# Opening of the stick-breaking stage reordered in a fused transformer layer

## The chip, the cores and the metric

The kernel runs on one core of a Trainium2 chip. Its time is the device time of one execution in microseconds (us), smaller is better. TensorE (PE) multiplies, VectorE (DVE), ScalarE (ACT) and GpSimd (POOL) work on tiles, and SyncE (SP) issues nearly all transfers, which run on 16 DMA engines. Each engine takes its instructions strictly in the order in which they were put down; engines wait for each other by semaphores.

## The reference, cut to what matters

One decoder layer on 1024 tokens of width 1024. The mixer has two attention families; the second, stick-breaking attention, is the place of the change, and the modulation vector `mod` is what the small weight tiles in it are for:

```python
mod = jax.nn.silu(c) @ ada_w[layer] + ada_b[layer]
shift1, scale1, gate1, shift2, scale2, gate2 = ...split(mod, 6)
...
# stick-breaking, 8 heads, blocks of 128 queries
z = einsum('bqhd,bshd->bhqs', qb, k) * scale
log_keep = where(mask, log_sigmoid(-z), 0.0)
suffix = cumsum(log_keep, reverse=True) - log_keep
a = where(mask, exp(log_sigmoid(z) + suffix), 0.0)
y_b = einsum('bhqs,bshd->bqhd', a, v)
...
h = h + gate1 * ((sigmoid(m_a) * y_a + sigmoid(m_b) * y_b) @ w_out)
h = h + gate2 * (square(relu(u2 @ mlp_w1)) @ mlp_w2)
```

All products are made from float32 values split into a high and a low part, so one product is three matmuls.

## The kernel before, in words

The program is one long stream: normalisation and input projection, sparse attention (`nsa_all`), stick-breaking attention (`sb_gens`), up-projection, output projection, MLP. A part of the input projection, 28 units of 48 matmuls of 128x512 (line L748, called filling products below, written to the banks `pd`), is kept back and laid between the matmuls of both attention stages, so that PE has work while their other engines are busy. `drive` draws filling products in proportion to the estimated cost of each attention step, `pump` draws a stretch of them at once. Finished units are copied out (`zo`, L1023) and stored to `z_d` in memory, from which the stick-breaking stage and the up-projection load them again.

The stick-breaking stage works head by head. For head h, `prep` loads its query and key rows (`zr`), casts the query tile `Q` on ACT (L1080), makes its low part and the key tiles `Kh`, `Kl` on POOL. `prep_v` takes the value rows of two heads (`vr`), transposes them on PE (L1098), casts them to `V` on ACT (L1102) and makes the low part on DVE (L1104). Then come twelve score chunks per head, in three groups of four (`sb_a`): two or three matmuls into a score bank `psx` (L1128 to L1131), a sigmoid into `sig` and a sigmoid in place on ACT (L1133, L1134), a running product from right to left on DVE into `Pt` (L1143), a multiplication on POOL (L1145). There are three banks `psx`, so the matmuls of chunk n+3 wait for the running product of chunk n. One group later the results are transposed on PE (`turn`, L1160), split on ACT and DVE (L1168, L1169) and multiplied with `V` (L1180).

`ada_rest(sp, (3,), ...)` makes one row of `mod` on the side: 32 steps, each loading a 128x256 tile `adraw` of `ada_w` on SP (L423), scaling it on ACT (L443) and adding it on POOL (L447). A buffer of `adraw` is free again after the addition. `side(1)` asks for one step; the first call only issues as many loads as there are buffers.

The order within each engine is not the order of the code alone: when the program is built, a scheduler plays it through on estimated times and lets any instruction that it thinks ready go ahead on its engine. The manual dependence in `behind` holds filling products behind the attention matmuls, and is off while `pump` runs.

Of the kernel before, what the change touches and what calls it, by code (L numbers as in the profile page):

```python
# [6 lines left out]
F32 = mybir.dt.float32  # L7
F32R = mybir.dt.float32r
BF16 = mybir.dt.bfloat16
AF = mybir.ActivationFunctionType  # L10
# [25 lines left out]
def build(tc, I, out):  # L36
    nc = tc.nc
# [65 lines left out]
    def po(name="po"):  # L103
# [7 lines left out]
                            fill=0.0, base=0, channel_multiplier=1)  # L111
    ones = const.tile([128, 128], F32, name="ones")
# [301 lines left out]
    def ada_rest(pool_, rows, ahead, engines, W=512):  # L414
        groups = [(r, h) for r in rows for h in range(D // W)]
        total = len(groups) * NK
        nxt = []

        def load(n):
            r, h = groups[n // NK]  # L420
            raw = pool_.tile([128, W], F32, name="adraw", bufs=ahead)
            c0 = (2 + r) * D + h * W
            nc.sync.dma_start(raw, ada_k[:, n % NK, c0:c0 + W])  # L423
            nxt.append(raw)

        for n in range(min(ahead, total)):
            load(n)
        yield
        for n in range(total):
            raw = nxt.pop(0)  # L430
            k = n % NK
            (r, h), w, e = groups[n // NK], cs[:, k:k + 1], engines[n // NK % len(engines)]
            if k == 0:
                acc = pool_.tile([128, W], F32, name="adacc", bufs=1)
            if e == "v":
                if k == 0:
                    nc.vector.tensor_scalar(acc, raw, w, None, op0=OP.mult)
                else:
                    nc.vector.scalar_tensor_tensor(acc, raw, w, acc, op0=OP.mult, op1=OP.add)
            else:  # L440
                d = acc if k == 0 else raw
                if e == "s":
                    nc.scalar.mul(d, raw, w)  # L443
                else:
                    nc.gpsimd.tensor_scalar(d, raw, w, 0.0, op0=OP.mult, op1=OP.add)
                if k:
                    nc.gpsimd.tensor_tensor(acc, acc, raw, op=OP.add)  # L447
            if n + ahead < total:
                load(n + ahead)
            if k == NK - 1:  # L450
                nc.sync.dma_start(acc_d[r][:, h * W:(h + 1) * W], acc)
            yield

    adp = pool("adp", "left")
    ada_steps = ada_rest(adp, (1, 2), 2, "v")

    def side(n):
        for _ in range(n):
            next(ada_steps, None)
# [269 lines left out]
    def track(ins):  # L729

        last[:] = [ins.ins]
# [7 lines left out]
    def unit_mm(w, sink):  # L739
        wh, wl = w  # L740
        pend = None
        for h in range(2):
# [3 lines left out]
            for k in range(NK):  # L746
                for n, (a, b) in enumerate(((wh[:, k], uH(k, sl)), (wh[:, k], ul[:, k, sl]), (wl[:, k], uH(k, sl)))):
# [4 lines left out]
                    if m == 3 and pend:  # L752
# [13 lines left out]
                            fill=NEG, base=0, channel_multiplier=-1)  # L766
# [6 lines left out]
                            fill=NEG, base=0, channel_multiplier=1)  # L773
# [240 lines left out]
    TAIL = 96  # L1014
# [24 lines left out]
    def drive(main, fill, ratio, extra=0.0, keep=0):  # L1039

        debt = 0.0
        for c in main:
            debt += c * ratio + extra
            while debt > 0 and left[0] > keep:
                m = next(fill, None)
                if m is None:
                    break
                debt -= m

    def pump(fill, us):  # L1050

        free[0] = 1
        while us > 0:
            m = next(fill, None)
            if m is None:
                break
            us -= m
        free[0] = 0


    def sb_gens(sp):
        zero = sp.tile([128, 128], F32, name="zero")[:, 0:1]
        nc.vector.memset(zero, 0.0)

        def load(u, h):
            zr = sp.tile([128, S], F32, name="zr", bufs=2)
            for r in range(2):
                nc.sync.dma_start(zr[r * HD:(r + 1) * HD], z_d[u][(h % 2) * HD:(h % 2 + 1) * HD, :])
            return zr

        def load_v(p):
            vr = sp.tile([128, S], F32, name="vr", bufs=1)
            nc.sync.dma_start(vr, z_d[8 + p])
            return vr
# [16 lines left out]

        def prep_v(vr, V):
            tv = [sp.tile([128, NT, 2, HD], F32R, name="V", bufs=3) for _ in range(2)]
            for q in range(2):
# [11 lines left out]
                yield 0.0  # L1106
            V.extend(tv)

# [62 lines left out]

        def times_v(V):
            h, g, kt, c0, th, tl = split_.pop(0)
# [5 lines left out]
            for q, t_ in enumerate((th, tl)):  # L1179
                track(nc.tensor.matmul(p[:, c0:], V[h][:, kt].rearrange("p s d -> p (s d)"), t_[:, c0:],  # L1180
                                       start=kt == top and q == 0, stop=kt == 0 and q == 1, skip_group_check=True))
# [8 lines left out]
        def sb_all():  # L1190
            lds = {0: (load(0, 0), load(4, 0))}
            vr = load_v(0)
            ops = {}
            for r in prep(0, lds[0]):
                ops[0] = r
            V = []
            for c in prep_v(vr, V):
                yield c
            groups = [(h, kind) for h in range(8) for kind in range(3)]
            A, edges, late = {}, {}, []  # L1200
            extra = []
            for k in range(len(groups) + 1):
                if k < len(groups):
                    h, kind = groups[k]
                    if kind == 0:
                        A[h, 0] = {}
                        if h + 1 < 8:
                            lds[h + 1] = (load((h + 1) // 2, h + 1), load(4 + (h + 1) // 2, h + 1))
                            if h % 2 == 1:
                                vr = load_v((h + 1) // 2)  # L1210
                    if kind == 1:
                        A[h, 1] = {}
                        if h + 1 < 8:
                            extra.append(prep(h + 1, lds[h + 1]))
                            if h % 2 == 1:
                                extra.append(prep_v(vr, V))
                    chunks = chunks_of(kind)
                for c in range(4):
                    cost = 0.0
                    if k < len(groups):  # L1220
                        fin, cost = sb_a(kind, chunks[c], ops[h], A[h, min(kind, 1)], edges)
                        late.append(fin)
                        yield cost
                    if len(late) > 1 or k == len(groups):
                        if late:
                            late.pop(0)()
                    cost = 0.0
                    if k > 0:
                        hb, kb = groups[k - 1]
                        g = min(kb, 1)  # L1230
                        cost += turn(hb, g, (3, 7, 3)[kb] - c, A[hb, g])

                        if split_ and (wait[0] or split_[0][2] != 4 * split_[0][1] + 3):
                            while len(split_) > 0:
                                cost += times_v(V)
                            wait[0] = 0
                        elif split_:
                            wait[0] = 1
                        if len(turned) > 1:
                            halves()  # L1240
                    yield cost
                    if c % 2:
                        side(1)
                    for e in list(extra):
                        r = next(e, "end")
                        if r == "end":
                            extra.remove(e)
                        elif isinstance(r, tuple):
                            ops[h + 1] = r
                        elif r:  # L1250
                            yield r
                if k < len(groups) and kind == 2:
                    for e in extra:
                        for r in e:
                            if isinstance(r, tuple):
                                ops[h + 1] = r
                            elif r:
                                yield r
                    extra = []
            while turned or split_:  # L1260
                cost = 0.0
                while split_:
                    cost += times_v(V)
                if turned:
                    halves()
                yield cost
# [78 lines left out]
    fill = fill_all()  # L1345
    pump(fill, 25.0)
    drive(nsa_all(), fill, 0.4, 0.05)
    pump(fill, 20.0)
    close(at)
    close(bnp)  # L1350
    close(kvp)
    sp = pool("sb", "right")
    ada_steps = ada_rest(sp, (3,), 2, "s", 256)
    drive(sb_gens(sp), fill, 0.55, 0.08, TAIL)
    for _ in ada_steps:
        pass
    close(sp)
# [39 lines left out]
    ada_steps = ada_rest(yb, (0,), 2, "s")  # L1397
# [367 lines left out]
```

## Time and profile before

| | us |
|---|---|
| median of three runs (lowest 1712.92, highest 5434.21) | 1713.28 |
| the profiled execution | 1711.0 |
| its span, first to last instruction | 1709.3 |
| PE busy in it | 1646.8 |
| DVE, POOL, ACT busy | 1276.9, 948.8, 875.7 |

The profiled execution is 1.7 us longer than its span; the median is 2.3 us above the profiled execution. The profile's times count from the start of the span. A PE busy for 96% of the span can gain from a change off PE only where it stands still or where its granted clock is down.

### The profile page before, as it was taken

What the parts mean: (1) busy time and instruction counts of PE and PEld (TensorE: products, weight loads), DVE (VectorE), ACT (ScalarE), POOL (GpSimd) and SP (SyncE); (2) the same over time, 40 slices, a digit from 0 to 9 for tenths busy, and PEclk for the clock granted to TensorE, in tenths of its full rate; (3) what the DMA queues carried; (4) which work ended last, traced back from release to release, by engine and by line L of the source; (5) the groups of instructions that cost most, each with busy time, mean ns of one, the idle gap of its engine ahead of it and who ended that gap; (6) DMA issues with size and microseconds to landing.
All of it is one profiled execution on the core that took longest, in us unless ns stands there. A gap on an engine that the chain in (4) does not pass through costs nothing.

```text
span 1709.3 us, 25308 instructions
## 1 busy us (share of the span) xinstructions
PE 1646.8 (96%) x8484; PEld 1384.8 (81%) x8484; DVE 1276.9 (75%) x2614; ACT 875.7 (51%) x1898; POOL 948.8 (56%) x837
## 2 busy tenths in 40 slices
PE   5999999999999989999999999899999999999998
PEld 4879888888888877878778888778788888888886
DVE  7598477778877648778745546679888888979887
ACT  6434376666666547776554435543444443453442
POOL 0021134343434368775316302399889897989897
PEclk9999999999999999999999999999999999999999
DMA  9366311111211164451187443865373654636232
GB/s 306 106 177 177 97 56 55 57 55 50 61 45 50 38 180 126 114 139 51 38 287 235 155 176 116 279 232 211 119 273 104 243 200 157 243 116 269 99 148 99
DMA packets 159386, 245.22 MB, mean 143 GB/s; under 512 B 15432, under 2 KB 109336, under 8 KB 150296
## 3 DMA queue, kind: packets, MB, share of 16 engines
q1 hardware_dynamic: 155032, 241.51, 42.6%
q10 hardware_dynamic: 4224, 2.10, 0.4%
q8 instruction: 67, 1.10, 0.3%
q14 instruction: 63, 0.52, 0.1%
HBM read 203.71 MB, written 39.86 MB: 142 GB/s over the span
## 4 chain that ended last, share of the span: by engine, by line
PE 75%; POOL 7%; DVE 6%; DMA 5%; ACT 3%; issue 3%; SPq 0%; POOLq 0%; DVEq 0%; ACTq 0%
PE pd L748 16%; PE psx L1705 10%; PE pd L1639 7%; PE pt L1639 5%; PE px L1329 5%; PE po L913 5%; PE px L1441 4%; PE pt L947 4%; PE po L1705 3%; POOL raw L1679 3%; DMA adraw<-in_ada_w_dram 2%; PE psx L829 2%; PE psx L830 2%; PE po L1180 1%; POOL wbl L1681 1%
## 5 line engine op out<-in xcount | busy, mean ns | idle before, releaser
L1708 DVE TENSOR_TENSOR acc<-acc,psx 128x512 f32<-128x512 f32 x288 | 178.8, 675 | 8.0 <-PE psx L1705 7.9
L748 PE MATMUL pd<-uh,uwh 128*128 128x512 f32 x448 | 181.4, 405 | 0.7 <-ACT zo L1023 0.7
L748 PE MATMUL pd<-ul,uwh 128*128 128x512 f32 x448 | 178.0, 397 | 0.0
L748 PE MATMUL pd<-uh,uwl 128*128 128x512 f32 x448 | 177.0, 395 | 0.0
L66 DVE TENSOR_TENSOR wl<-aw,wh 128x1024 fp32r<-128x1024 f32 x49 | 115.1, 2349 | 65.8 <-ACT wh L61 65.8
L1679 POOL TENSOR_TENSOR raw<-r 128x512 f32<-128x512 f32 x80 | 131.3, 1659 | 32.1 <-ACT r L1614 32.0
L1705 PE MATMUL psx<-wbl,rah 128*128 128x512 f32 x336 | 131.3, 391 | 4.2 <-POOL wbl L1681 3.0
L1705 PE MATMUL psx<-wbh,rah 128*128 128x512 f32 x336 | 130.8, 391 | 1.9 <-ACT wbh L1680 1.5
L1705 PE MATMUL psx<-wbh,ral 128*128 128x512 f32 x336 | 131.0, 390 | 0.1
L905 DVE TENSOR_TENSOR tl<-pt,th 128x512 fp32r<-128x512 f32 (+8 forms) x168 | 103.6, 619 | 34.5 <-ACT th L904 33.4
L1681 POOL TENSOR_TENSOR wbl<-raw,wbh 128x1024 fp32r<-128x1024 f32 x40 | 109.1, 2728 | 19.5 <-ACT wbh L1680 19.5
L904 ACT CAST th<-pt 128x512 fp32r<-128x512 f32 (+8 forms) x168 | 88.7, 530 | 61.0 <-PE pt L947 59.0
L886 POOL TENSOR_TENSOR pcx<-pcx,tot 128x64 f32<-128x64 f32 (+7 forms) x32 | 10.5, 329 | 172.2 <-DVE tot L884 95.3
L63 POOL TENSOR_SCALAR uwh<-uwr 128x512 fp32r<-128x512 f32 x54 | 33.5, 628 | 123.2 <-PE pd L748 96.7
L1667 POOL TENSOR_TENSOR w<-w,grow 128x1024 f32<-128x1024 f32 x32 | 95.0, 2991 | 11.8 <-DVE aw L1595 11.8
L748 PEld LDWEIGHTS pd<-uh,uwl 128*128 128x128 f32 x448 | 85.0, 190 | 17.8
L1680 ACT CAST rah<-raw 128x1024 fp32r<-128x1024 f32 x40 | 41.4, 1050 | 111.7 <-PE po L1705 58.8
L748 PEld LDWEIGHTS pd<-uh,uwh 128*128 128x128 f32 x448 | 85.3, 190 | 14.9 <-ACT zo L1023 1.1
L748 PEld LDWEIGHTS pd<-ul,uwh 128*128 128x128 f32 x448 | 85.3, 190 | 13.2
L1639 PE MATMUL pd<-mth,wl 128*128 128x512 f32 x224 | 87.6, 392 | 0.8 <-DVE wl L66 0.8
L1639 PE MATMUL pd<-mth,wh 128*128 128x512 f32 x224 | 87.8, 392 | 0.6 <-ACT wh L61 0.6
L1639 PE MATMUL pd<-mtl,wh 128*128 128x512 f32 x224 | 87.8, 392 | 0.0
(361 smaller groups left out, 5352.5 us busy)
## 6 DMA issues: line engine op xcount, KB each, us to landing
mtl<-t_d SPq DMA_DIRECT2D x35, 1024.0 KB, 5.8
mth<-t_d SPq DMA_DIRECT2D x35, 1024.0 KB, 8.2
w<-in_mlp_w_dram SPq DMA_DIRECT2D x32, 512.0 KB, 6.1
z_d<-zo SPq DMA_DIRECT2D x56, 256.0 KB, 2.0
aw<-in_mlp_w_dram SPq DMA_DIRECT2D x28, 512.0 KB, 4.2
uwr<-in_w_in_dram SPq DMA_DIRECT2D x54, 256.0 KB, 3.0
adraw<-in_ada_w_dram SPq DMA_DIRECT2D x48, 256.0 KB, 3.0
xa<-in_ada_w_dram SPq DMA_DIRECT2D x32, 256.0 KB, 5.7
```

What stands on the lines that cost most here:

```text
L66: (nc.vector if e == "v" else nc.gpsimd).tensor_tensor(dst, src, f(h), op=OP.subtract)
L748: r = nc.tensor.matmul(p, a, b, start=(k == 0 and n == 0), stop=(k == NK - 1 and n == 2))
L904: nc.scalar.copy(th[:rows, :w], p[:rows, :w])
L905: nc.vector.tensor_tensor(tl[:rows, :w], p[:rows, :w], f(th)[:rows, :w], op=OP.subtract)
L913: track(nc.tensor.matmul(po_[:, :256], w, tt[q][:rows, m * 256:(m + 1) * 256], start=(n == 0 and m == 0 and q == 0), stop=(n == last and m ...
L1329: nc.tensor.matmul(p, a, b, start=(k == 0 and n == 0), stop=(k == 3 and n == 2))
L1639: nc.tensor.matmul(bank[ft], a[:, k, fs], b[k], start=(k == 0 and m == 0 and not on), stop=(k == 3 and m == 2), skip_group_check=on)
L1667: nc.gpsimd.tensor_tensor(W2[c][j], W2[c][j], grow2, op=OP.mult)
L1679: nc.gpsimd.tensor_tensor(d, block(i0, j0, s), block(i1, j1, s), op=OP.add if sg > 0 else OP.subtract)
L1681: (nc.vector if e == "v" else nc.gpsimd).tensor_tensor(l.rearrange("p s n -> p (s n)"), src, f(h).rearrange("p s n -> p (s n)"), op=OP.sub ...
L1705: nc.tensor.matmul(p, a[:, s, qs], b[:, s], start=(s == 0 and n == 0), stop=(s == 1 and n == 2))
L1708: nc.vector.tensor_tensor(acc[:, t, ds_], acc[:, t, ds_], p, op=OP.add if sg > 0 else OP.subtract)
```

## The change

The stage is opened in steps. The filling products that were drawn in one stretch of 20 us ahead of the stage are drawn as 4 us ahead of it, 8 us after the first head's query and key preparation, and 8 us after the value preparation, which is now written in one piece. Right after the first loads are issued, a sigmoid of one column (`warm`) is written, so that the table of sigmoid is loaded there. The modulation row has eight buffers `adraw` where it had two; its first loads are issued with the value preparation, and the group of the first head's first four chunks asks for no steps.

```diff
-        zero = sp.tile([128, 128], F32, name="zero")[:, 0:1]
+        zero = sp.tile([128, 128], F32, name="zero")
+        warm, zero = zero[:, 1:2], zero[:, 0:1]
         nc.vector.memset(zero, 0.0)
...
             vr = load_v(0)
+
+            nc.scalar.activation(warm, ones[:, 0:1], AF.Sigmoid)
             ops = {}
             for r in prep(0, lds[0]):
                 ops[0] = r
+            yield 0.0
             V = []
             for c in prep_v(vr, V):
-                yield c
+                pass
+            side(1)
+            yield 0.0
...
-                    if c % 2:
+                    if k > 0 and c % 2:
                         side(1)
...
-    pump(fill, 20.0)
+    pump(fill, 4.0)
...
-    ada_steps = ada_rest(sp, (3,), 2, "s", 256)
-    drive(sb_gens(sp), fill, 0.55, 0.08, TAIL)
+    ada_steps = ada_rest(sp, (3,), 8, "s", 256)
+    sb = sb_gens(sp)
+    for us in (8.0, 8.0):
+        next(sb)
+        pump(fill, us)
+    drive(sb, fill, 0.55, 0.08, TAIL)
```

On ACT, from the last step of sparse attention to the second score chunk, the order before is this (`sig_...` with its number is one tile of `sig`):

```order
L960 COPY otmp<-po 64x256
L1023 COPY zo<-pd 128x512
L1080 CAST Q<-zr 128x1024
L1023 COPY zo<-pd 128x512
L443 ACTIVATE adacc<-adraw,cs 128x256
L443 ACTIVATE adraw<-adraw,cs 128x256
L1080 CAST Q<-zr 128x1024
L443 ACTIVATE adraw<-adraw,cs 128x256
L1102 CAST V<-pt 128x4x64 x2
L443 ACTIVATE adraw<-adraw,cs 128x256
L1102 CAST V<-pt 128x4x64 x2
L1133 ACT_TABLE_LOAD
```

After the change the same stretch of ACT reads:

```order
L1195 ACT_TABLE_LOAD
L1195 ACTIVATE zero<-ones 128x1
L1023 COPY zo<-pd 128x512
L1081 CAST Q<-zr 128x1024
L443 ACTIVATE adacc<-adraw,cs 128x256
L1023 COPY zo<-pd 128x512
L443 ACTIVATE adraw<-adraw,cs 128x256 x7
L1103 CAST V<-pt 128x4x64 x4
L1081 CAST Q<-zr 128x1024
L1134 ACTIVATE sig_8461<-psx 128x512
L1135 ACTIVATE psx<-psx 128x512
L443 ACTIVATE adraw<-adraw,cs 128x256 x2
```

The table load moved ahead of the copy `zo`; eight scalings of `adraw` in place of four stand ahead of the first sigmoid, and two more between the first chunk's sigmoids and the second's.

On SP, from the first loads of the stage on, the order before is:

```order
L1068 DMA zr<-z_d 64x1024 x4
L1024 DMA z_d<-zo 128x512 x2
L1073 DMA vr<-z_d 128x1024
L710 DMA uwr<-in_w_in_dram 128x4x128 x2
L423 DMA adraw<-in_ada_w_dram 128x256 x2
L1068 DMA zr<-z_d 64x1024 x2
L1024 DMA z_d<-zo 128x512
L710 DMA uwr<-in_w_in_dram 128x4x128
L423 DMA adraw<-in_ada_w_dram 128x256
L1068 DMA zr<-z_d 64x1024 x2
```

And after (`uwr` is the raw weight of a filling unit, whose buffer is free after the DVE instruction on `uwl`, L66):

```order
L1069 DMA zr<-z_d 64x1024 x4
L1024 DMA z_d<-zo 128x512
L1074 DMA vr<-z_d 128x1024
L1024 DMA z_d<-zo 128x512
L423 DMA adraw<-in_ada_w_dram 128x256 x8
L1069 DMA zr<-z_d 64x1024 x2
L1024 DMA z_d<-zo 128x512
L710 DMA uwr<-in_w_in_dram 128x4x128 x2
L1069 DMA zr<-z_d 64x1024 x2
L423 DMA adraw<-in_ada_w_dram 128x256 x4
```

Eight loads of `adraw` now go out in one row ahead of the second head's first `zr`, and the next four stand behind two `uwr` and two `zr`.

On PE, at the first score chunks, four transposes of `vr` stood three filling products ahead of the first score matmul before; now all eight stand 16 filling products ahead of it, and the rows between the chunks read, in the changed kernel:

```order
L1132 MATMUL psx<-diagr,identr 128x128
L748 MATMUL pd<-ul,uwh 128x512
L748 MATMUL pd<-uh,uwl 128x512
L1129 MATMUL psx<-Kh,Q 128x128
L1130 MATMUL psx<-Kl,Q 128x128
L1132 MATMUL psx<-diagr,identr 128x128
L1129 MATMUL psx<-Kh,Q 128x512
L1130 MATMUL psx<-Kl,Q 128x512
L1132 MATMUL psx<-diagr,identr 128x128
L748 MATMUL pd<-uh,uwh 128x512
```

The fourth chunk (128x128) and the fifth still follow each other with no filling product between them.

## Rows read from the trace of the kernel before

**Rows 1.** The page's busy times, share of the span and instructions of each engine.

```profile
PE 1646.8 (96%) x8484; PEld 1384.8 (81%) x8484; DVE 1276.9 (75%) x2614; ACT 875.7 (51%) x1898; POOL 948.8 (56%) x837
```

**Rows 2.** Stretches: length, busy PE, PEld, DVE, ACT, POOL, granted clock, DMA, GB/s.

```profile
625.70:630.94 5.24, 0.00 (x0) 0.00 (x1) 2.03 (x4) 4.72 (x10) 4.33 (x4) 0.82 0.98 301
630.94:635.68 4.74, 4.74 (x14) 3.94 (x15) 3.22 (x7) 3.92 (x10) 4.36 (x7) 0.50 0.58 151
...
642.70:645.20 2.50, 0.81 (x6) 0.40 (x4) 2.50 (x5) 1.27 (x6) 0.90 (x1) 1.00 0.80 192
645.20:650.00 4.80, 4.80 (x18) 4.02 (x19) 4.80 (x12) 3.89 (x9) 4.72 (x6) 0.64 0.10 35
650.00:856.00 206.00, 196.59 (x1071) 163.04 (x1070) 156.89 (x304) 137.38 (x318) 131.84 (x139) 0.98 0.34 94
...
892.00:895.30 3.30, 3.30 (x9) 2.61 (x8) 1.11 (x2) 0.72 (x1) 3.30 (x3) 0.50 0.84 254
```

**Rows 3.** PE in order of time: start, length, instruction, idle time before and releaser.

```profile
622.28 0.39 PE L1128 MATMUL psx<-Kh,Q 128*128 128x512 f32 x1
...
625.30 0.39 PE L748 MATMUL pd<-uh,uwl 128*128 128x512 f32 x1
630.94 0.47 PE L1128 MATMUL psx<-Kh,Q 128*128 128x128 f32 x1 [5.25 <-DVE Pt L1143]
...
644.28 0.33 PE L1128 MATMUL psx<-Kh,Q 128*128 128x128 f32 x1 [1.23 <-DVE Pt L1143]
...
645.18 0.50 PE L1128 MATMUL psx<-Kh,Q 128*128 128x512 f32 x1 [0.47 <-DVE Pt L1142]
...
891.18 0.50 PE L1329 MATMUL px<-oh,wh 128*128 128x512 f32 x1 [2.62 <-ACT wh L61]
```

**Rows 4.** ACT in order of time, at the opening of the stage.

```profile
607.46 0.58 ACT L1023 COPY zo<-pd 128x512 f32<-128x512 f32 x1 [3.74 <-PE pd L748]
...
619.71 0.51 ACT L443 ACTIVATE adacc<-adraw,cs 128x256 f32<-128x256 f32 x1 [5.20 <-DMA adraw<-in_ada_w_dram]
...
621.63 1.05 ACT L1080 CAST Q<-zr 128x1024 fp32r<-128x1024 f32 x1 [1.01 <-DMA zr<-z_d]
...
626.19 0.51 ACT L443 ACTIVATE adraw<-adraw,cs 128x256 f32<-128x256 f32 x1 [1.54 <-DMA adraw<-in_ada_w_dram]
...
627.25 1.28 ACT L1133 ACT_TABLE_LOAD   x1
628.54 0.60 ACT L1133 ACTIVATE sig<-psx 128x512 f32<-128x512 f32 x1
```

**Rows 5.** SP's issues in order of time.

```profile
608.94 0.46 SPq L1073 DMA_DIRECT2D vr<-z_d  x1
...
611.02 1.07 SPq L423 DMA_DIRECT2D adraw<-in_ada_w_dram  x2
613.44 1.27 SPq L1068 DMA_DIRECT2D zr<-z_d  x2
...
618.08 0.39 SPq L710 DMA_DIRECT2D uwr<-in_w_in_dram  x1
```

**Rows 6.** The chain that ended last, in order of time: start, length, what.

```profile
594.13 3.41 PE pd L748 x15
...
611.02 8.66 DMA adraw<-in_ada_w_dram
...
621.86 4.25 DMA adraw<-in_ada_w_dram
```

**Rows 7.** DVE in order of time.

```profile
618.56 0.69 DVE L66 TENSOR_TENSOR uwl<-uwr,uwh 128x512 fp32r<-128x512 f32 x1 [0.51 <-POOL uwh L63]
...
640.61 2.41 DVE L66 TENSOR_TENSOR uwl<-uwr,uwh 128x512 fp32r<-128x512 f32 x2
```

**Rows 8.** Who waited for whom from 650 to 856 us: total, times, longest.

```profile
PE psx L1128 <- DVE Pt L1143: 4.8, 5, 1.3
...
ACT adraw L443 <- DMA adraw<-in_ada_w_dram: 10.2, 9, 2.6
```

## The prediction

> **What bounds the kernel now.** I read the page first: PE is busy for 1646.8 of 1709.3 us [rows 1], so only a stretch in which PE stands still or runs at a lower clock can give time back. Then the stretches around the opening of the stick-breaking stage [rows 2], and in them PE, ACT, SP and DVE in order of time. The place is 625.7 to 650 us, and it loses in four pieces.
>
> PE ends its last filling product at 625.7 and waits 5.25 us for the fourth score chunk [rows 3]. The fourth chunk needs the first of the three score banks back, so it waits for the first chunk's running product on DVE, and that for the two sigmoids on ACT. The first chunk's scores begin at 622.28 [rows 3], but its first sigmoid at 628.54 [rows 4]. Behind the pause PE runs from 630.94 to 635.68 at a granted clock of 0.50, the lower of its levels (1.2 in place of 2.4 GHz) [rows 2]: half of 4.74 us, 2.37 us. Then come two pauses of 1.23 and 0.47 us [rows 3], 1.7 us, and from 645.2 to 650 a clock of 0.64 [rows 2]: 0.36 x 4.80 = 1.73 us. Together 5.25 + 2.37 + 1.70 + 1.73 = 11.0 us. That is all that the opening can give back. The rest of the stage, 650 to 856 us, has 206.0 - 196.6 = 9.4 us in which PE is idle [rows 2].
>
> Why the first sigmoid is late stands in ACT's rows. ACT takes its instructions in order, and ahead of that sigmoid are four scalings of `adraw`, whose data come late: the first loads are issued at 611.02 and the first lands 8.66 us later [rows 6], ACT waits 5.20 us for it, later 1.54 us for the fourth [rows 4], then come the casts of `V` and the table load, 1.28 us [rows 4].
>
> **The change part by part.**
>
> *Table load.* It leaves the path from the first score chunk to the first sigmoid and goes ahead of the copy `zo` at 607.46. There ACT has idled 3.74 us [rows 4]; 1.28 us for the load and, for the one-column sigmoid, less than the 0.51 us of a 256-wide scaling [rows 4] fit. It costs nothing there, and it takes 1.28 us from the chain.
>
> The row has the table load at 627.25 for 1.28 us and the first sigmoid right behind it. The Trainium skill (ScalarE: Activation LUTs, "What ACT_TABLE_LOAD costs") gives about 1283 ns for the load and another 1380 ns of drain; this trace agrees on the first and shows no second. By the page the chain would lose 2.66 us and the opening would come out some 1.4 us better.
>
> *Values and filling products.* The same eight transposes and four casts run, earlier; the yields that drew about 6 filling products are gone, and these come later. The sum of PE's work is the same, so I take 0. On PE the score chunks begin about where they did: by PE's order 72 products and 8 transposes stand between the last matmul of sparse attention and the first chunk, against 76 and 8. Products follow each other at 3.41 / 15 = 0.23 us [rows 6], so the first chunk starts at about 622.28 - 4 x 0.23 = 621.4.
>
> *Eight buffers.* Now eight scalings stand ahead of the first sigmoid. Their loads go out when `vr` and the stores ahead are issued, at about 608.94 + 0.46 = 609.4, 0.54 us each (two take 1.07), and the second head's `zr` follow at 613.7, as they did at 613.44 [rows 5]. With the 8.66 us of [rows 6] for every load the eighth, issued at 613.2, lands at 621.9 at the latest; I take 618, since two `uwr` no longer stand ahead of them. Then the casts of `V`, and the cast of `Q`, which waits for `zr` as before and began at 621.63 [rows 4]: it ends near 622.5. So the first sigmoid starts at about 622.5 in place of 628.54. From its start to the fourth chunk took 630.94 - 628.54 = 2.40 us [rows 3, 4], which gives 624.9. PE had work for 625.69 - 622.28 = 3.41 us from its first chunk on [rows 3] and has two products less now, so until 621.4 + 2.95 = 624.3. First pause: 0.6 us.
>
> *The new wait.* Between the first chunk's sigmoids and the second's ACT now has two more scalings. Their loads stand on SP behind two `uwr`, whose second buffer comes free when DVE ends at 618.56 + 0.69 = 619.25 [rows 7], as far as DVE keeps its pace. One `uwr` 0.39, two `zr` 1.27 [rows 5], and one `adraw` 0.54: the two loads go out at about 621.4 and 621.9. At the 4.25 us of the load issued at 621.86 [rows 6] the second lands at 626.2; with the 0.51 us of a scaling [rows 4] the second chunk's sigmoid starts at 626.7. What is queued behind it on ACT is every further sigmoid; who waits is PE, for the fifth chunk, which follows the fourth directly. The second chunk is 384 wide where the first was 512, so I scale 2.40 to 1.9: the fifth chunk starts at 628.6, the fourth ends near 625.4. Second pause: 3.2 us. The two pauses make 3.8 us against 5.25, a gain of 1.45.
>
> *The clock.* The longest pause is now nearer to the 2.62 us before 891.18 [rows 3], which was followed by 3.30 us at 0.50 [rows 2], 1.65 us lost, than to the 5.25 us with its 2.37. Gain 0.7; with no lower clock at all it would be 2.37, with the old one 0.
>
> *Behind it.* Up to the eighth chunk the order has the same 90 products as before, but between the eighth and the twelfth it has none where it had 12, and six of them stand behind the twelfth. DVE still has the two splits of `uwl` there, 2.41 us for both [rows 7]. I charge six products, 6 x 0.23 = 1.4 us, as added pause; the bounds are 0, if DVE has run ahead, and 2.7 us for all twelve.
>
> *The rest of the stage.* With two buffers ACT waited 10.2 us in nine pieces for loads [rows 8]. With eight this goes. What of it PE felt is at most its waits for running products, 4.8 us [rows 8]; I take half, 2.4 us, since the score chunks also wait for DVE's own work. The 32 scalings and additions are the same in number, only earlier.
>
> Sum: 1.45 + 0.7 - 1.4 + 2.4 = 3.15, so about 3.2 us less. Made against the profiled execution that is 1711.0 - 3.2 = 1707.8; the median lies 2.3 us above it, so 1713.28 - 3.2 = **1710.1 us**.
>
> **The rivals.**
>
> *A: the new wait does not show.* If the two loads land by the end of the first chunk's sigmoids, ACT runs on, PE pauses only for tenths, and the clock stays up. For it speaks that the row of eight loads has fewer slow neighbours; against it that DMA is busy for 0.98 of the time from 625.7 to 630.9 [rows 2]. Then all 11.0 us go: 1702.3 us, and with the 2.4 us of the rest 1699.9.
>
> *B: slower, by the loads in front of ACT.* If the two loads behind `uwr` and `zr` take 8.66 us, as the first did [rows 6], they land at 630.6, the second chunk's sigmoid starts at 631.0 and the fifth chunk at 632.9: pauses of 0.6 + 7.5 = 8.1 us, 2.85 more than before. The clock gives nothing back, the 1.4 us behind it stay, and the rest gives nothing: 1713.28 + 4.25 = 1717.5 us. It decides from a landing at which the gain of the pauses is gone, 5.25 - 0.6 = 4.65 us of second pause, so at about 627.7, 5.8 us after issue. Between the 4.25 and the 8.66 of the rows, the nearer is the 4.25, which was issued at the same time with two `zr` ahead of it.
>
> The Trainium skill (DMA: Bandwidth & Descriptors, "Queues, rings and completion order") has each DMA engine take what was issued from one queue in ring order, which speaks against eight loads put ahead of `zr`. The 8.66 us of the load behind `vr` and two `uwr` agree with it; by that rule rival B is the more likely the fuller the queue is.
>
> *C: the gap only moves.* The change does on PE what it says, but what PE gains at the fourth chunk it loses up to the sixteenth, where the products missing between the chunks leave DVE's chain uncovered (2.7 us in place of 1.4), and the rest of the stage comes out as before. Then 1.45 + 0.7 - 2.7 is a loss of 0.55: 1713.8 us.
>
> **How the numbers follow.** The forecast, a gain between 1 and 7 us, gets 0.50; A 0.18; B 0.20; C 0.12. The range goes from 1702.3, the whole opening gone without the rest, to 1717.0, just under B. It leaves out the better half of A and the worse half of B, together some 0.2. Faster by over 2% would be under 1679 us and takes 34 us where the whole stage has 11.0 + 9.4 us of loss: 0.01. Slower by over 2% would need a pause of 34 us: 0.01. Within 2%, about what a measurement of this kernel can tell from no change: 0.98.
>
> **What would show it.** In the profile of the changed kernel: the table load near 604 to 605 with no wait behind it; the first score sigmoid near 622.5; PE's pause ahead of the fourth chunk under 1.5 us; a wait of ACT for `adraw` between the first and second chunk's sigmoids, 2 to 3 us, and PE's pause ahead of the fifth chunk. If ACT waits there under 0.5 us, A holds; if over 4 us, B. If PE pauses more around the twelfth chunk than 1.23 us, C has its price. I would be wrong altogether if the transposes of `vr` waited for its load and held PE, or if the copy of `zo`, now behind the first scaling, came so late that a filling product waited for its bank.

## The result, and the profile after

The changed kernel takes 1721.26 us (median of 10 runs, 1718.23 to 1730.58) against 1713.10 of before on the same chip. It is slower by 8.2 us by these medians and by about 10 us by the ratio of all executions (1.0059, interval 1.0044 to 1.0073; it leaves out the one of before that took 5434.21 us), where the forecast was 3.2 us faster. Its profiled execution took 1718.57 us, with a span of 1716.9 us.

The profile's busy times of the changed kernel answer to [rows 1]; PE's work is the same in number:

```profile
PE 1651.0 (96%) x8484; PEld 1385.6 (81%) x8484; DVE 1275.9 (74%) x2614; ACT 875.8 (51%) x1899; POOL 949.8 (55%) x837
```

ACT of the changed kernel in order of time, against [rows 4]:

```profile
603.97 0.37 ACT L960 COPY otmp<-po 64x256 f32<-64x256 f32 x1 [3.32 <-PE po L913]
604.36 1.28 ACT L1195 ACT_TABLE_LOAD   x1
605.65 0.20 ACT L1195 ACTIVATE zero<-ones 128x1 f32<-128x1 f32 x1
...
616.68 0.51 ACT L443 ACTIVATE adacc<-adraw,cs 128x256 f32<-128x256 f32 x1 [5.15 <-DMA adraw<-in_ada_w_dram]
...
622.70 0.60 ACT L1134 ACTIVATE sig<-psx 128x512 f32<-128x512 f32 x1
...
627.14 0.91 ACT L443 ACTIVATE adraw<-adraw,cs 128x256 f32<-128x256 f32 x2 [3.35 <-DMA adraw<-in_ada_w_dram]
627.96 0.47 ACT L1134 ACTIVATE sig<-psx 128x384 f32<-128x384 f32 x1
```

SP's issues, against [rows 5], and PE, against [rows 3]:

```profile
610.11 6.69 SPq L423 DMA_DIRECT2D adraw<-in_ada_w_dram  x8
616.90 1.09 SPq L1069 DMA_DIRECT2D zr<-z_d  x2
...
621.10 2.27 SPq L423 DMA_DIRECT2D adraw<-in_ada_w_dram  x4
```

```profile
621.99 0.39 PE L1129 MATMUL psx<-Kh,Q 128*128 128x512 f32 x1
...
625.11 0.33 PE L1129 MATMUL psx<-Kh,Q 128*128 128x128 f32 x1 [0.17 <-DVE Pt L1144]
...
629.85 0.80 PE L1129 MATMUL psx<-Kh,Q 128*128 128x512 f32 x1 [4.19 <-DVE Pt L1144]
...
640.75 0.39 PE L1129 MATMUL psx<-Kh,Q 128*128 128x256 f32 x1 [1.12 <-DVE Pt L1143]
...
642.59 0.33 PE L1129 MATMUL psx<-Kh,Q 128*128 128x128 f32 x1 [1.21 <-DVE Pt L1144]
```

The first chunks went as forecast: the table load costs nothing, the first sigmoid starts at 622.70, ACT waits for two late loads until 627.14, and PE's pause has moved from the fourth chunk to the fifth, 4.19 us in place of 5.25.

The loss is found by cutting the stage in two where the prediction stopped reading: from the end of the last `otmp` copy of sparse attention to the first matmul of the thirteenth score chunk (the opening; 645.18 in [rows 3]), and from there to the sixteenth and last store of `ob_d` (the rest). The stretches give length, busy PE, PEld, DVE, ACT, POOL, granted clock, DMA, GB/s. Before:

```profile
603.73:645.18 41.45, 33.84 (x156) 27.53 (x154) 21.62 (x39) 21.20 (x47) 28.23 (x27) 0.92 0.72 198
645.18:857.26 212.08, 202.66 (x1092) 168.13 (x1093) 162.39 (x316) 141.81 (x327) 136.58 (x144) 0.98 0.33 92
```

The changed kernel:

```profile
604.34:646.68 42.34, 34.96 (x151) 28.32 (x149) 23.34 (x42) 24.83 (x57) 32.52 (x32) 0.88 0.82 225
646.68:864.51 217.83, 203.97 (x1099) 166.76 (x1099) 160.49 (x313) 137.36 (x317) 130.72 (x140) 0.99 0.30 83
```

The opening is 0.9 us longer, the rest 5.75 us, and what follows the last store is equal (1709.3 - 857.26 = 852.0 and 1716.9 - 864.51 = 852.4). The lengths mislead a little, since six filling products have moved behind the cut (93 begin in the opening, against 99), at 0.227 us each by [rows 6] 1.4 us of PE's time. Length less busy time, PE's idle time, is the clearer measure: in the opening 7.4 us against 7.6 before, in the rest 13.9 against 9.4. So up to the twelfth chunk PE stands still as long as before, and behind it 4.4 us longer. In the rest the waits of the changed kernel:

```profile
ACT th L1169 <- PE pt L1161: 43.0, 25, 4.4
DVE tl L1170 <- ACT th L1169: 27.4, 20, 3.2
DVE Pt L1144 <- ACT psx L1135: 11.2, 24, 1.1
PE psx L1129 <- DVE Pt L1144: 8.9, 13, 1.6
ACT adraw L443 <- DMA adraw<-in_ada_w_dram: 6.0, 7, 1.9
```

and of before:

```profile
ACT th L1168 <- PE pt L1160: 32.9, 29, 3.0
DVE Pt L1143 <- ACT psx L1134: 22.2, 31, 3.0
DVE tl L1169 <- ACT th L1168: 17.0, 22, 2.5
ACT adraw L443 <- DMA adraw<-in_ada_w_dram: 10.2, 9, 2.6
PE psx L1128 <- DVE Pt L1143: 4.8, 5, 1.3
```

ACT waits less for `adraw`, as forecast, though 6.0 of the 10.2 us stay. But PE waits 13 times for a running product where it waited 5 times. ACT waits longer for PE's transposes, and DVE for ACT's copies of them, while DVE waits less for the sigmoids. PE and the two others take turns in waiting for each other, which is what badly spread filling products would do; the waits alone do not prove it. PE's order shows the spread; filling products ahead of each of chunks 13 to 36:

```
before    0 0 6  0 0 6 0 12  0 0 6 0   12 0 0 12 0  6 0 0 24 0 0 6
changed   6 0 0 12 0 0 0  6 24 0 0 0    0 0 6  6 0 12 0 0 24 0 0 6
```

The changed kernel has 24 products ahead of the 21st chunk and then five chunks with none. PE pauses on this bare row, at the 24th and the 25th chunk, where before has no pause for a score chunk:

```profile
670.13 0.33 PE L1129 MATMUL psx<-Kh,Q 128*128 128x128 f32 x1 [1.59 <-DVE Pt L1144]
...
671.04 0.50 PE L1129 MATMUL psx<-Kh,Q 128*128 128x512 f32 x1 [0.47 <-DVE Pt L1144]
```

Nobody wrote this order: six products fewer were drawn at the opening, and the scheduler laid the rest of the stage differently.

### The profile page after: what moved, and what is told of

The parts are those of the page before. It is cut to its first block, busy times and chain, and to the rows that moved or that the text cites. A ratio compares the mean times of both kernels' runs of the same rounds, so it can differ in the third digit from the quotient of the medians.

```text
span 1716.9 us, 25308 instructions
## 1 busy us (share of the span) xinstructions
PE 1651.0 (96%) x8484; PEld 1385.6 (81%) x8484; DVE 1275.9 (74%) x2614; ACT 875.8 (51%) x1899; POOL 949.8 (55%) x837
## 4 chain that ended last, share of the span: by engine, by line
PE 74%; POOL 8%; DVE 6%; DMA 5%; issue 4%; ACT 3%; SPq 0%; POOLq 0%; DVEq 0%; ACTq 0%
PE pd L748 16%; PE psx L1715 10%; PE pd L1649 7%; PE pt L1649 5%; PE px L1335 5%; PE po L913 4%; PE px L1451 4%; PE pt L947 4%; PE po L1715 3%; POOL raw L1689 3%; PE psx L829 2%; PE psx L830 2%; PE cb L304 1%; POOL wbl L1691 1%; PE pt L1161 1%
## 5 line engine op out<-in xcount | busy, mean ns | idle before, releaser
L66 DVE TENSOR_TENSOR wl<-aw,wh 128x1024 fp32r<-128x1024 f32 x49 | 114.8, 2342 | 66.5 <-ACT wh L61 66.5
L1689 POOL TENSOR_TENSOR raw<-w,w 128x512 f32<-128x512 f32 x48 | 87.2, 1837 | 0.5
```

The source lines that it names most:

```text
L66: (nc.vector if e == "v" else nc.gpsimd).tensor_tensor(dst, src, f(h), op=OP.subtract)
L1689: nc.gpsimd.tensor_tensor(d, block(i0, j0, s), block(i1, j1, s), op=OP.add if sg > 0 else OP.subtract)
```

## The experiments

The ratio is to before on the same chip, whose median there was between 1710.64 and 1713.10 us. The next three columns are from each kernel's one profiled execution: "stage" is the length of opening and rest together less before's 253.53 us, the two "idle" columns are PE's idle time in the opening and in the rest, where before has 7.6 and 9.4 us. "Thin" counts in PE's order, from the 13th chunk on, how often five chunks in a row have six products or fewer; before has 5.

| kernel | median us | ratio, interval | stage | idle, opening | idle, rest | thin |
|---|---|---|---|---|---|---|
| changed | 1721.26 | 1.0059 (1.0044, 1.0073) | +6.6 | 7.4 | 13.9 | 7 |
| e1 | 1711.58 | 0.9997 (0.9985, 1.001) | -0.7 | 7.1 | 9.4 | 5 |
| e2 | 1711.79 | 1.001 (0.9999, 1.002) | -1.1 | 9.3 | 9.7 | 6 |
| e3 | 1724.87 | 1.0081 (1.0067, 1.0096) | +10.8 | 8.2 | 16.4 | 7 |
| e4 | 1723.54 | 1.0076 (1.0061, 1.0092) | +11.8 | 7.1 | 16.5 | 7 |
| e5 | 1712.38 | 1.0008 (0.9999, 1.0017) | -2.4 | 6.6 | 9.5 | 3 |
| e6 | 1709.49 | 0.9989 (0.9979, 0.9998) | -3.6 | 6.7 | 9.9 | 4 |
| e7 | 1716.69 | 1.0035 (1.0021, 1.0049) | +5.0 | 8.7 | 10.9 | 6 |
| e8 | 1709.24 | 0.9991 (0.9981, 1.0002) | -4.1 | 6.7 | 10.5 | 2 |
| e9 | 1718.53 | 1.0031 (1.002, 1.0042) | +4.8 | 8.3 | 12.3 | 4 |
| e10 | 1713.65 | 1.001 (0.9999, 1.0021) | +0.7 | 4.4 | 14.8 | 1 |
| e11 | 1720.60 | 1.0039 (1.0023, 1.0054) | +4.2 | 7.9 | 12.9 | 9 |
| e12 | 1706.01 | 0.9958 (0.9945, 0.9971) | -6.2 | 5.0 | 9.9 | 3 |
| e13 | 1722.15 | 1.0054 (1.0041, 1.0067) | +8.9 | 4.9 | 17.6 | 7 |
| e14 | 1712.19 | 0.9995 (0.9984, 1.0006) | -2.4 | 8.3 | 9.4 | 6 |
| e15 | 1708.71 | 0.998 (0.9969, 0.999) | -4.5 | 4.8 | 10.2 | 4 |
| e16 | 1713.80 | 1.0008 (0.9998, 1.0019) | -0.1 | 6.3 | 11.0 | 6 |

The stage column lies between 3.8 us below and 1.0 us above what the ratio makes of 1713 us. Kernels with the same order on PE agree in the idle time of the rest within 0.3 us (before and e1, e2 and e14, e3 and e4), in that of the opening within 1.0 us.

### Which part: e1 to e4

Theory O: the loss comes with the moved values and the split pump, by PE's order. B: by the eight buffers. P: any small shift of the schedule does it.

**e1**, before with the early table load alone:

```diff
+            nc.scalar.activation(warm, ones[:, 0:1], AF.Sigmoid)
```

> The kernel before with only the one-column sigmoid and its table load put first; the order on PE and the rest of ACT is that of before. Theory O (the loss of the changed kernel comes from the order of matmuls and filling products on PE that the moved values and pumps bring): a gain, about 1.3 us of PE's 5.25 us pause at the fourth chunk, so 1711 to 1713 against 1713. Theory B (it comes from the eight buffers, whose loads and scalings hold ACT): the same here. Theory P (any small shift of the schedule moves this stage by several us, either way): the same too, since the order stays.

**e2**, before with eight buffers alone:

```diff
+    ada_steps = ada_rest(sp, (3,), 8, "s", 256)
```

> The kernel before with only eight buffers for the modulation tiles; by the order ten scalings stand ahead of the first sigmoid instead of four, PE's order is nearly that of before. Theory O: within 2 us of before, 1711 to 1716. Theory B: slower by 5 us or more, 1718 and up. Theory P: anything within 4 us of before.

**e3**, before with the values in one piece and the pump in three, and **e4**, the changed kernel with two buffers again:

```diff
-                yield c
+                pass
...
+    for us in (8.0, 8.0):
+        next(sb)
+        pump(fill, us)
```

> The kernel before with only the values moved between pumped products (20 us drawn as 4, 8 and 8, and the values' steps no longer drawing products of their own); two buffers, table load in its old place. PE's order is that of the changed kernel. Theory O: 6 to 9 us slower than before, 1719 to 1722. Theory B: as fast as before or faster, 1708 to 1714. Theory P: within 4 us of before.

> The changed kernel with two buffers again: values moved and table load first. Theory O: 4 to 8 us slower than before, 1717 to 1721, the table load giving back about one us against the values alone. Theory B: 3 to 6 us faster than before, 1707 to 1710. Theory P: within 4 us of before.

Table and buffers alone change nothing that can be measured. The moved values alone cost 0.8%, so O holds against B and P, though e3 and e4 lie 2.5 to 3 us above its ranges. Eight buffers take some of the idle time back, 13.9 us in the rest against the 16.5 of e4; by the times that gain is not clear of the noise. With two, ACT of e3 stands 4.99 us at one load and PE 3.63 us behind it,

```profile
729.11 0.51 ACT L443 ACTIVATE adraw<-adraw,cs 128x256 f32<-128x256 f32 x1 [4.99 <-DMA adraw<-in_ada_w_dram]
```

```profile
731.83 0.49 PE L1180 MATMUL po<-th,V 128*128 128x512 f32 x1 [3.63 <-ACT th L1168]
```

where the same wait of PE in the changed kernel's rest is 0.5 us.

### The moved transposes, or the products that are not drawn: e5 to e8

**e5**, e3 with the drawing given back behind the values:

```diff
+            yield 4 * PT_
+            yield 0.0
+            yield 4 * PT_
```

> The kernel before with the values and the three pumps moved as in the change (which alone cost 13 to 14 us, 1724.9 against 1711.0), and with eight 128-wide transposes' worth of drawing given back right behind them, so that the stage draws its six filling products again. Theory D (the loss comes from the six products that the values' yields no longer draw, so that every later score chunk has fewer products ahead of it): about the time of before, 1709 to 1713 us. Theory M (the loss comes from moving the transposes and splitting the pump, whatever is drawn): still 1722 to 1726 us. Theory P (any shift of the count of products against the chunks gives another time, without order): a time of its own between 1708 and 1726, with both other theories missed by more than 3 us.

**e6**, before, whose values stay but draw nothing:

```diff
             for c in prep_v(vr, V):
-                yield c
+                pass
```

> The kernel before, in which the values' transposes keep their place and the pump stays in one piece, but their steps draw no filling products. Theory D: the loss appears, 1721 to 1726 us. Theory M: no loss, 1709 to 1713 us. Theory P: anything from 1708 to 1726, not bound to what e5 gives.

**e7**, the changed kernel with `for us in (8.0, 9.3)`:

> The changed kernel with its last pump 9.3 us long in place of 8.0, so that six filling products more stand ahead of the first score chunks and of nearly all later ones. Theory D: the loss is gone and the opening is at most 1 to 3 us better, 1708 to 1712 us. Theory M: still 1719 to 1723 us. Theory P: any time in 1708 to 1726.

**e8**, before with `pump(fill, 18.7)`:

> The kernel before with a pump of 18.7 us in place of 20.0: six filling products fewer ahead of the first score chunk, nothing else edited. Theory D: it loses as the change does, 1719 to 1726 us. Theory M: like before, 1709 to 1713 us. Theory P: a change of over 3 us either way, not the same as e6, though the counts of products ahead of most chunks are the same in both.

M falls: with the values moved, e5 is back at before. D falls as well: by PE's order e6 and e8 have six products fewer than before ahead of most chunks and lose nothing. e7 gives back less than half by the ratio. So neither the transposes nor the number decide; P is left, and P predicts nothing. The count of thin rows was made as a rule to be tried on further orders.

### Where the products lie: e9 to e12

**e9**, the changed kernel with the six products given back as in e5:

> The whole changed kernel, with the six filling products that the values' steps no longer draw given back behind them, as e5 did without the table and the buffers. Theory S (what costs is where later products fall among the score chunks: how often five chunks in a row have six products or fewer between them, counted from the 13th chunk in PE's order: before 5 times, changed kernel 7, e5 3, e6 4, e7 6, e8 2): this order has 4, so 1708 to 1713 us. Theory T (the table and the early values cost by themselves once they come together, as e7 with six products more stayed 5.9 us above before): 1716 to 1722 us.

**e10** and **e11**, the changed kernel and before, each with the same single edit:

```diff
-    drive(..., fill, 0.55, 0.08, TAIL)
+    drive(..., fill, 0.65, 0.08, TAIL)
```

> The changed kernel with products drawn at 0.65 of each step's cost in place of 0.55, so that the last score chunk has 1248 products ahead of it in place of 1212; nothing else edited. By theory S its order has only 1 row of five thin chunks, against 7 in the changed kernel: 1705 to 1712 us. Theory T: the opening is the same, so at least half of the loss stays, 1716 to 1722 us. Theory C (what counts is only how many products have been drawn): better than the changed kernel by the same amount as e11 is better than before.

> The kernel before with the same single edit as e10, 0.65 in place of 0.55. By theory S its order has 9 rows of five thin chunks, against 5 before: slower than before by 5 to 15 us, 1716 to 1726 us, though e10 gains by the same edit. Theory C: the same sign and about the same amount as e10 against the changed kernel, so 1700 to 1708 us. Theory T says nothing on it, about 1711 us.

**e12**, e8 with the early table load and the eight buffers:

> The kernel before with a pump of 18.7 us (e8), and of the change only the early table load and the eight buffers; the values stay where they were and draw. Rows of five thin chunks: 3. Theory S: 1706 to 1711 us, no more than 3 us from e8, since neither edit moves PE's order. Against it: if the table and the buffers open the stage as forecast for them, about 4 to 6 us less than e8, 1703 to 1705 us.

The same edit takes the changed kernel's ratio from 1.0059 to 1.001 and before's from 1 to 1.0039. That kills theory C and is what S had said in sign, with e11 inside its range and e10 1.7 us above it. But e10 does not gain where S looks: PE stands still 3.0 us less than in the changed kernel in the opening and 1.0 us more in the rest, with a single thin row there.

e9 misses S by 5 us and lies in the range of T. With as many matmuls as before up to the thirteenth chunk, its opening takes 44.85 us against 41.45, 3.4 of the 4.8 us of its loss. With six products more, the scheduler put three more scalings of `adraw` ahead of the first sigmoid on ACT, and both they and the second `Q` wait for loads:

```profile
626.39 1.05 ACT L1081 CAST Q<-zr 128x1024 fp32r<-128x1024 f32 x1 [2.70 <-DMA zr<-z_d]
...
629.35 1.30 ACT L443 ACTIVATE adraw<-adraw,cs 128x256 f32<-128x256 f32 x3 [1.91 <-DMA adraw<-in_ada_w_dram]
630.57 0.57 ACT L1134 ACTIVATE sig<-psx 128x512 f32<-128x512 f32 x1
```

The first sigmoid comes 24.1 us after the start of the stage, against 18.36 us in the changed kernel. So the edits at the opening gain something only on some orders; that much of T is right.

e12 beats both kernels, before by 0.42%. By the ratios that is 5.7 us less than e8, by the medians 3.2 us; S allowed 3 us, and the rival beside it had forecast 4 to 6. So on nearly e8's order table and buffers are worth something. Its stretches, opening and rest:

```profile
609.14:646.84 37.70, 32.70 (x150) 26.61 (x148) 20.38 (x38) 22.78 (x52) 27.60 (x27) 0.91 0.82 222
646.84:856.51 209.67, 199.79 (x1101) 165.67 (x1100) 165.14 (x317) 140.15 (x323) 136.54 (x144) 1.00 0.33 92
```

### New orders, and the new wait: e13 to e16

**e13**, the changed kernel with twelve buffers:

> The changed kernel with twelve buffers for the modulation tiles in place of eight: their loads go out in one row, and on ACT no scaling stands any more between the first chunk's sigmoids and the second's. PE's order is that of the changed kernel but for six products in the second head (rows of five thin chunks 7, as in it). If the new wait costs what the trace shows at the fifth chunk, 4.19 us, and nothing takes its place: 3 to 4 us less than the changed kernel, 1717 to 1718.5 us. If the wait only moves ahead of the first sigmoid, since twelve loads in a row land later: 1720 to 1723 us. Under 1714 us would mean that the opening and not the later order holds the loss, against theory S.

**e14**, before with table load and eight buffers:

> The kernel before with the early table load and the eight buffers together, values and pump as they were; PE's order differs from before in six products of one head. Theory S: no loss, within 2 us of before, 1710 to 1713 us. If the two together open the stage better, as e12 was 3 us below e8: 1707 to 1710 us. Theory T (table and early loads cost once together): 1715 us or more.

**e15**, the changed kernel with `for us in (8.0, 8.65)`:

> The changed kernel with its last pump 8.65 us long in place of 8.0, three filling products more. Its PE order has 4 rows of five thin chunks against 7 in the changed kernel and 5 in before. Theory S: at least 5 us of the loss gone, 1709 to 1715 us. Theory T: as the changed kernel, 1718 to 1722 us.

**e16**, before with `pump(fill, 21.3)`:

> The kernel before with a pump of 21.3 us in place of 20.0, six filling products more ahead of the first chunk. Its PE order has 6 rows of five thin chunks, and 11 places with twelve products or fewer over six chunks, against 5 and 7 in before. Theory S: slower than before by 2 to 6 us, 1714 to 1718 us. Theory C (the more products drawn ahead, the better) or T: 1709 to 1712 us.

e15 decides against T: with all edits in place, three filling products more at the opening take 12.5 us by the medians from the changed kernel and make it faster than before, by 0.2%. Its stretches:

```profile
603.53:644.06 40.53, 35.73 (x163) 28.92 (x161) 21.82 (x39) 24.03 (x56) 30.82 (x30) 0.92 0.83 237
644.06:852.52 208.46, 198.26 (x1087) 164.30 (x1087) 162.31 (x316) 139.11 (x319) 134.22 (x141) 0.99 0.32 87
```

PE stands still 2.6 us less than in the changed kernel in the opening and 3.7 us less in the rest. In the opening its ninth to twelfth chunk have 6, 6, 0 and 6 products ahead where the changed kernel has none. Its first sigmoid starts 22.93 us after the start of the stage, later than the 18.36 us of the changed kernel, so an early first sigmoid is not what makes a good opening:

```profile
626.46 0.58 ACT L1134 ACTIVATE sig<-psx 128x512 f32<-128x512 f32 x1
```

e16 lies just under what S expected and its interval touches no change, so it tells little; e14 shows no gain on before's order.

In e13 the wait only moves: PE stands still 2.5 us less than in the changed kernel in the opening and 3.7 us more in the rest. Twelve loads go out in one row, the `zr` behind them late, and PE pauses at the fourth chunk and, 5 us behind the thirteenth, at a transpose:

```profile
608.55 8.20 SPq L423 DMA_DIRECT2D adraw<-in_ada_w_dram  x12
...
617.32 2.38 SPq L1069 DMA_DIRECT2D zr<-z_d  x4
```

```profile
626.83 0.33 PE L1129 MATMUL psx<-Kh,Q 128*128 128x128 f32 x1 [3.47 <-DVE Pt L1144]
...
644.77 0.45 PE L1161 MATMUL pt<-ident,sigr 128*128 128x128 f32 x1 [3.98 <-DVE Pt L1143]
```

How far the rule of thin rows goes: the four kernels with 7 (changed, e3, e4, e13) have 13.9 to 17.6 us of idle PE in the rest, but their orders are nearly one and the same. Those with 2 to 6 have 9.4 to 12.3 us, e11, with 9, has 12.9, and e10, with 1, has 14.8 and contradicts the rule. It is a rough sign, not a law. Nor is it shown that PE's order is what costs: the scheduler's orders for ACT, DVE and SP change with it, and no run holds them fixed.

## Why the prediction was wrong

The step that failed is in *Values and filling products*: "The sum of PE's work is the same, so I take 0." The sum is the same, but six products moved at the opening set another order for the seven heads behind it, and that was priced at nothing; the order was read up to the twelfth chunk only. Behind it PE stands still 4.4 us longer than before. e3 shows the cost alone (+0.8%, 7.0 us more of idle PE in the rest); e5 and e15 take it away again by the count of products.

Of the gain of 0.75 us forecast for the opening (1.45 + 0.7 - 1.4), 0.2 us came as idle time. By its other steps (the stamps of the changed kernel lie 0.6 us later by themselves, since its stage began at 604.34 in place of 603.73):

- *Table load*: right. 1.28 us at 604.36, no wait behind it, and the next instruction 0.01 us after its end. The Trainium skill's further 1380 ns of drain (ScalarE: Activation LUTs, "What ACT_TABLE_LOAD costs") does not show in this row either. By itself it is worth nothing that can be measured (e1: 0.9997, interval 0.9985 to 1.001).
- *Eight buffers*: first sigmoid forecast at 622.5, measured 622.70, in part by luck. An issue of `adraw` took 6.69 / 8 = 0.84 us in place of 0.54, so the `zr` left at 616.90 and not at 613.7; yet the second `Q` did not wait for them, as forecast, but followed the scalings and the casts of `V` without a pause.
- *The new wait*: right in place. The two scalings start at 627.14 against a landing forecast at 626.2, the fifth chunk at 629.85 against 628.6. Pauses of 0.17 + 4.19 us against 0.6 + 3.2.
- *The clock*: forecast 0.7 us back. Behind the pause of 4.19 us PE ran at a granted clock of 0.50, the level of 1.2 GHz, for 5.82 us, against 4.74 in [rows 2], so nothing came back:

```profile
629.85:635.67 5.82, 5.82 (x15) 4.67 (x16) 2.19 (x4) 2.61 (x7) 5.22 (x6) 0.50 1.11 243
```

- *Behind it*: 1.4 us forecast for the missing products at the ninth to twelfth chunk; the two pauses there are 1.12 + 1.21 us against the 1.23 + 0.47 of [rows 3], 0.6 us more. In the opening of e15, which has products there, PE stands still 2.6 us less, though not for this alone.
- *The rest*: 2.4 us of gain forecast, 5.75 us of loss measured (4.4 us of it idle PE). The mechanism named there exists on the order with moved values, where eight buffers take the idle PE of the rest from 16.5 us (e4) to 13.9, though that order differs a little from the changed kernel's. It was outweighed. On nearly before's order (e2, e14) it gains nothing: PE's idle time in the rest is 9.7 and 9.4 us, against 9.4.

Rival C, the gap only moves, had the sign and a part of the mechanism, products missing between chunks, but looked for it up to the sixteenth chunk and gave 0.5 us. Rival B's price hung on a landing past 627.7; it was about 627.1, so B did not happen.

What stays open: of the 6.6 us by which the stage is longer, 4.2 us is PE's idle time, and 2.4 us stands as busy PE (238.9 us against 236.5), for the same work and at the same granted clock of 0.97 over the stage. PE waits oftener; whether each break of the matmul pipeline costs time that the modelled ends hide was not tried. And which feature of the later order costs the time is not known, since the rule of thin rows fails on e10.

## What to carry to other kernels

Where a scheduler lays work around filler, an edit that changes how much filler is drawn is an edit of the whole stage: read the order to its end and look for bunches followed by bare rows. Tell the edit from its phase by shifting the filler alone, by a few products each way, in both kernels; here that moved the time from 1708.7 to 1721.3 us with the same edits in place. And compare stage lengths and idle times, not stamps.

## What was not expected of the hardware

The code ahead of the stage is the same in every kernel here, yet the stage began between 602.25 us (e11) and 609.14 us (e12) after the start of the span. e12 has the lowest median although its profiled stage began 5.4 us later than before's. One execution's time is thus no measure of a stage. Its length from a mark at its start is a better one: the three pairs with the same order on PE agree within 0.7 to 1.4 us (the table's column "stage").

With eight buffers on nearly before's order PE stands still longer (19.1 us over the stage in e2, 17.7 in e14, against 17.0), and yet the profiled stage is 1.1 and 2.4 us shorter. PE's busy time fell for the same work, from 236.5 us to 233.4 in both, at a granted clock of 0.98 over the stage against 0.97. So a part of a shorter stage can be the clock alone.
